# A model's expert stage: the main up projection is ordered behind a rare branch, and the branch hint is issued later

## The chip, the cores and the metric

The kernel runs on one core of one Trainium2 chip. The metric is the device time of one execution, in microseconds (us). PE is TensorE (matmuls; PEld are its weight loads), DVE is VectorE, ACT is ScalarE, POOL is GpSimd, SP is SyncE, whose queue issues the weight transfers here. "PEq" or "SPq" is the instruction queue (the sequencer) of that engine.

## The reference

Two transformer stacks run one after the other on 256 tokens of width 1024. The first has four layers of three kinds of mixers, the second one hybrid mixer and one layer of experts. Only the experts matter here:

```python
def clamped_swiglu(hgu):
    gate, up = jnp.split(hgu, 2, axis=-1)
    gate = jnp.minimum(gate, SWIGLU_LIMIT)
    up = jnp.clip(up, -SWIGLU_LIMIT, SWIGLU_LIMIT)
    return gate * jax.nn.sigmoid(SWIGLU_ALPHA * gate) * (up + 1)

logits = (xt @ w_router + b_router).astype(jnp.float32)
top_v, top_e = lax.top_k(logits, TOP_K)            # 4 of 32 experts for each token
gates = jax.nn.softmax(top_v, axis=-1)
# for each expert e, over the tokens that chose it:
y_e = clamped_swiglu(x @ w1[e] + b1[e]) @ w2[e] + b2[e]     # w1[e]: 1024 x 2048, w2[e]: 1024 x 1024
# the sum over a token's four experts, weighted by its gates, is added to the stream, then a norm
```

With 256 tokens and 4 choices of 32, an expert gets 32 tokens on average; the number depends on the data.

## The kernel before, in words

All of it is one program of straight code. The mixers fill about the first 1300 us; the expert stage (`route`, then `experts`) fills the rest, and the change is there.

**Weights.** An expert's weights are 12 transfers of 1024 KB: eight chunks of `w1` (128 rows each) and four of `w2`. `wload` issues them on SP's queue in a fixed order: the eight of `w1[e+1]`, then the four of `w2[e]`, and so on. They go into a ring of 18 buffers (`SPLIT + sum(RING) + 4`), so each load takes the buffer that was filled 18 loads before, and can start only when the last reader of that buffer is done. Counted through, the loads 3 to 6 of `w1[e+2]` take the buffers of `w2[e-1]`, its loads 7 and 8 those of the first two chunks of `w1[e+1]`, the four of `w2[e+1]` those of chunks 3 to 6 of `w1[e+1]`, and the first two of `w1[e+3]` those of its chunks 7 and 8.

**One expert.** For expert e the code (the loop at L1924) calls `others`, then `up_proj`, the main up projection for the first 64 tokens: 8 chunks x 4 column blocks, 32 matmuls into the sums `hg` (a bias had been written there by `new_hg`). `swiglu` runs on DVE and ACT. Then `down` of the expert before (16 matmuls into `py`), then `between`: the bias of the next expert (4 matmuls on `sel`), `prep` (a gather matmul of the tokens for the next pair of experts, into a tile `g`, whose result DVE and ACT scale into `xq`; at odd experts also slot gates and transposes of `P`), and `act_T`, four transposes of the activation. At even experts a `scatter` of 8 matmuls adds the pair's result to the stream.

**The branch.** Tokens beyond the 64th of an expert are rare. `others(e)` (L1895) is a runtime branch on the number `more`: its body does the down projection of the rest of expert e-2 and the up projection of the rest of expert e, with further conditions inside. The body reads `w1[e]` and `w2[e-2]` once more. Each engine takes the branch for itself: it loads the number into a register and jumps over the body where it is 64 or less. `branch_ahead` (L1705) places the load, and for PE a hint that this jump is coming; it is called in `down_proj`, behind the matmul `kk == hh == 0`, for the expert after the next.

**What sets the order.** A scheduler orders each engine's instructions by their dependences. `up_proj` does not depend on the body (the body writes other sums, the two tiles `hg0` and `hg1`), and so the scheduler may put its matmuls ahead of the branch, and does. A buffer counts as free behind its last reader in the program: for a chunk that is read by `up_proj` ahead of the branch that is the body, and so the branch's end.

Of the kernel before, what the change touches and what calls it, by code (L numbers as in the profile page):

```python
# [51 lines left out]
def tile_model(ctx: ExitStack, tc: tile.TileContext, A, out):  # L52
# [18 lines left out]
    ps = psst.enter_context(tc.tile_pool(name="ps", bufs=2, space=PSUM))  # L71
# [8 lines left out]
    ident = cb[:, 0:128]  # L80
# [54 lines left out]
    def mm(o, l, r, start=True, stop=True):  # L135
        return T.matmul(o, l, r, start=start, stop=stop)  # L136
# [1271 lines left out]
    def w2_tile(e, kk, hh):  # L1408

        if e < 31:  # L1410
            return w2s[e][kk // 2][:, kk % 2, hh * 512:(hh + 1) * 512]
        return w2s[e][2 * hh + kk // 4][:, kk % 4, :]
# [138 lines left out]
    def slices(j):  # L1551
        return slice(64 * j, 64 * j + 64)
# [3 lines left out]
    def block(hg, b):  # L1556
        if len(hg.shape) == 2:
            return hg[32 * b:32 * b + 32, :], 32
        return hg[64 * (b % 2):64 * (b % 2) + 64, b // 2, :], 64
# [10 lines left out]
    def ytile():  # L1570
        return rt["pe"].tile([128, 512], F32, name="py", tag="py", bufs=2)
# [58 lines left out]
    def experts(pos, gate, num, more):  # L1630
        h = xc
        with ExitStack() as st:
# [30 lines left out]
            def onehots(P, e, s0=0):  # L1663

                for t in range(2):
                    at = pos[:, t, e:e + 1]
                    if s0:
                        ats = ep.tile([128, 1], F32, name="ats", tag="ats")
                        V.tensor_scalar(ats, at, -float(s0), None, ALU.add)
                        at = ats  # L1670
                    V.tensor_scalar(P[:, t], slots, at, None, ALU.is_equal)  # L1671

            def gather(P, n, dst, ks, ps=None):

                w = n * 64
                step = min(512 // w, ks[1] - ks[0])
                for k0 in range(ks[0], ks[1], step):
                    p = (gtile() if ps is None else ps).rearrange("p (a b) -> p a b", b=w)
                    for t in range(2):
                        for k in range(k0, k0 + step):  # L1680
                            mm(p[:, k - k0, :], h[:, t, k * 128:(k + 1) * 128], P[:, t, :], t == 0 and k == k0, t == 1 and k == k0 + step - 1)
                    modulate(dst[:, k0:k0 + step, :], p, range(k0, k0 + step))
# [19 lines left out]
            def branch_ahead(after, i):  # L1702

                with tc.issue_after(after.ins):
                    conds[i] = nc.values_load(more[0:1, i - 1:i], min_val=0, max_val=256)  # L1705
                    tc.mark_branch_hint_location(f"more{i}", "LikelyTaken", [mybir.EngineType.PE])

            def up_proj(w1, hg, xs, k0=0, k1=8):
                for k in range(k0, k1):
                    for b in range(4):  # L1710
                        i = mm(block(hg, b)[0], xs[:, k, :], w1[k][:, b * 512:(b + 1) * 512], False, k == 7)
                return i
# [17 lines left out]
            def down_proj(aT, e, gs, take):  # L1730

                p = ytile()
                for kk in range(8):
                    for hh in range(2):
                        i = T.matmul(p[64 * hh:64 * hh + 64, :], aT[:, kk % 4, 64 * (kk // 4):64 * (kk // 4) + 64],  # L1735
                                     w2_tile(e, kk, hh), start=kk == 0, stop=kk == 7)
                        if kk == hh == 0:
                            branch_ahead(i, e + 2)
                for hh in range(2):
                    sl = slice(hh * 512, (hh + 1) * 512)  # L1740
                    rs = slice(64 * hh, 64 * hh + 64)
                    take(sl, p[rs, :], gs[rs], g2[rs])
                return i
# [12 lines left out]
            def new_P1():  # L1756
                return ep.tile([128, 512], F32, name="P1", tag="gm")[:, 0:128].rearrange("p (a b) -> p a b", b=64)
# [8 lines left out]
            def gather_more(e, j, ps):  # L1766
                P1 = new_P1()
                onehots(P1, e, 64 * j)
                gather(P1, 1, xs1, (0, 8), ps)

            def up_more(e, hgs, g, k0=0, k1=8):
                if k0 == 0:
                    bias(e, hgs[g])
                up_proj(w1s[e], hgs[g], xs1[:, :, 32 * g:32 * g + 32], k0, k1)

            def act_more(hgs, g, um):
                swiglu(hgs[g][0:64], hgs[g][64:128], um[half(g)], half(g))
# [46 lines left out]
            def prepare_sum(q):  # L1824
                gs = ep.tile([128, 2], F32, name="gsq", tag="gsq", bufs=2)
                slot_gates(Pq[q], 2 * q, gs)
                gTs[q] = (twice(30, F32R) if q == 15 else new_gT(F32R), gs)
                if q < 15:
                    transposed(Pq[q], gTs[q][0])
# [33 lines left out]
            def count(e):  # L1863
                return nc.values_load(num[0:1, e:e + 1], min_val=0, max_val=256)

            def down_others(e, ps):

                n, ums = count(e), umss[e % 2]
                with tc.If(n > 64):
                    down_more(e, 1, 0, ums[:, 0], ps)  # L1870
                    with tc.If(n > 96):
                        down_more(e, 1, 1, ums[:, 0], ps)
                        with tc.If(n > 128):
                            for j in (2, 3):
                                for g in range(2):
                                    down_more(e, j, g, ums[:, j - 1], ps)

            def up_others(e, ps):

                n, ums = count(e), umss[e % 2]  # L1880
                with tc.If(n > 64):
                    gather_more(e, 1, ps[1])
                    up_more(e, ps, 0)
                    act_more(ps, 0, ums[:, 0])
                    with tc.If(n > 96):
                        up_more(e, ps, 1)
                        act_more(ps, 1, ums[:, 0])
                        with tc.If(n > 128):
                            for j in (2, 3):
                                gather_more(e, j, ps[1])  # L1890
                                for g in range(2):
                                    up_more(e, ps, g)
                                    act_more(ps, g, ums[:, j - 1])

            def others(i, downs, ups):  # L1895

                ps = [pe.tile([128, 512], F32, name=f"hg{g}", tag=f"hg{g}") for g in range(2)]
                m = conds[i] if i else count(0)
                with tc.If(m > 64, label=f"more{i}"):
                    for e in downs:  # L1900
                        down_others(e, ps)
                    for e in ups:
                        up_others(e, ps)

            umss = [ep.tile([128, 3, 512], F32, name=f"ums{i}", tag=f"ums{i}") for i in range(2)]

# [16 lines left out]
            hg = rt["hg"]  # L1923
            for e in range(32):  # L1924
                while len(w1s.get(e, ())) < 8:
                    wload()
                others(e, (e - 2,) if e > 1 else (), (e,))
                i = up_proj(w1s[e], hg, xq[e // 2][:, :, slices(e % 2)])
                if e == 0:
                    prepare_sum(0)  # L1930
                    branch_ahead(i, 1)
                um = ep.tile([128, 512], F32, name="um", tag="um")
                swiglu(hg[:, 0], hg[:, 1], um)
                def between():

                    nxt = new_hg(e + 1) if e < 31 else None
                    if e < 30:
                        prep(e // 2 + 1, e % 2)
                    return nxt, act_T(um)

                if e == 0:
                    hg, aT = between()
                else:
                    last = down(e - 1, aT)
                    with tc.issue_after(last.ins):
                        hg, aT = between()
                    if e % 2 == 0:
                        scatter(gTs.pop(e // 2 - 1)[0], yes.pop(e // 2 - 1))
                    if e == 20:
                        add_b2()  # L1950
                    if e == 30:
                        ends = prepare_end()
# [33 lines left out]
            ps = [ytile() for _ in range(2)]  # L1986
            prod(0, range(8), ps[0])

            hg = rt["pe"].tile([128, 2, 512], F32, name="hg", tag="hg")
# [11 lines left out]
            i = V.scalar_tensor_tensor(yl[:, 1], ps[1], gs[:, 1:2], g2f[:, 512:1024], ALU.mult, ALU.mult)  # L2001
# [21 lines left out]
    r = route()  # L2023
    ph1.close()
    experts(*r)


# [182 lines left out]
```

## Time and profile before

| | us |
|---|---|
| median of 3 runs (lowest, highest) | 2420.92 (2414.31, 2422.75) |
| the profiled execution, device time | 2417.13 |
| its span | 2415.3 |
| PE busy in the span | 2259.0 (94%) |
| DVE, ACT, POOL busy | 1186.6, 725.8, 81.4 |

PE is busy 94% of the span. A matmul's busy time overlaps its neighbours', so that lengths of work are better read from one start to the next. The mean granted TensorE clock over the span is 0.967 of full speed. In all, 576 MB are moved, nearly all of them weights.

### The profile page before, as it was taken

To read this page: it belongs to the slowest core of one execution; us is meant where nothing else is said; L and a number is where in the kernel's file an instruction comes from. 1 tells how busy PE (TensorE), PEld (TensorE's weight loads), DVE (VectorE), ACT (ScalarE), POOL (GpSimd) and SP (SyncE) were. 2 spreads that over 40 slices of the span, in tenths; PEclk is the share of its full clock that TensorE was granted. 3 is DMA by queue.
4 is the path that set the end of the run, shared out by engine and by line. 5 is a ranking of instruction groups with operands and counts; after the bars stand their busy time and mean duration, and the time that the engine had idled before them with its cause. 6 is when DMAs were issued, how large, how long until landed. Compare 5 with 4: busy or idle time off the path is not lost. (4 is left out here: it accounts for less than half of the span.)

```text
span 2415.3 us, 32552 instructions
## 1 busy us (share of the span) xinstructions
PE 2259.0 (94%) x12508; PEld 1360.8 (56%) x12508; DVE 1186.6 (49%) x2549; ACT 725.8 (30%) x1588; POOL 81.4 (3%) x125
## 2 busy tenths in 40 slices
PE   7999999999999999999999999997988988998887
PEld 4767777777788887668865343332433333433332
DVE  4877666656666668867544323232322333432223
ACT  3545454444333455654223101010110101111001
POOL 0000010000000010002200000000000000000000
PEclk9999999999999999999989999898999989999999
DMA  8443432333333245456227978696999868999996
GB/s 304 131 144 131 135 119 74 108 134 110 118 105 112 81 129 187 167 198 244 82 89 285 413 301 348 263 366 241 416 415 415 332 276 326 367 416 416 415 380 247
DMA packets 124792, 576.08 MB, mean 239 GB/s; under 512 B 11953, under 2 KB 12721, under 8 KB 91762
## 3 DMA queue, kind: packets, MB, share of 16 engines
q1 hardware_dynamic: 124530, 572.71, 62.2%
q8 instruction: 149, 2.44, 0.4%
q14 instruction: 113, 0.93, 0.1%
HBM read 571.61 MB, written 1.05 MB: 237 GB/s over the span
## 5 line engine op out<-in xcount | busy, mean ns | idle before, releaser
L136 PE MATMUL hg<-w,xq 128*64 128x512 f32 x2048 | 505.7, 607 | 42.6 <-DMA w<-w 20.1
L136 PE MATMUL mm<-hT,wp 128*128 128x256 f32 (+1 forms) x1776 | 352.9, 342 | 0.5 <-DVE aqk L144 0.5
L136 PEld LDWEIGHTS hg<-w,xq 128*64 128x64 f32 x2048 | 149.4, 138 | 328.7 <-issue 290.9
L136 PEld LDWEIGHTS mm<-hT,wp 128*128 128x128 f32 x1776 | 270.1, 190 | 64.0 <-issue 27.8
L1735 PE MATMUL py<-w,aT 128*64 128x512 f32 x992 | 230.3, 599 | 20.7 <-DMA w<-w 20.7
L111 DVE TENSOR_TENSOR wp<-w,wp 128x1024 fp32r<-128x1024 f32 (+2 forms) x149 | 178.1, 1200 | 67.1 <-ACT wp L110 66.0
L1716 DVE TENSOR_SCALAR gm<-hg 128x512 f32<-128x512 f32 (+1 forms) x37 | 25.5, 690 | 372.0 <-PE hg L136 369.8
L136 PE MATMUL mm<-wp,hT 128*128 128x256 f32 (+1 forms) x1584 | 199.2, 284 | 4.0 <-DVE mixT L406 2.5
L136 PEld LDWEIGHTS mm<-wp,hT 128*128 128x128 f32 x1584 | 192.0, 190 | 11.9 <-DVE mixT L406 2.7
L110 ACT ACTIVATE wp<-w 128x1024 fp32r<-128x1024 f32 (+2 forms) x149 | 153.8, 1035 | 86.2 <-PE mm L136 57.7
L1735 PEld LDWEIGHTS py<-w,aT 128*64 128x64 f32 x992 | 80.1, 138 | 167.7 <-issue 122.5
L1717 ACT ACTIVATE um<-gm 128x512 f32<-128x512 f32 x32 | 20.2, 630 | 441.0 <-DVE gm L1716 441.0
L136 PE MATMUL ada<-w,scT 128*32 128x512 f32 x576 | 117.7, 620 | 8.0 <-DMA w<-l_w_ada 4.5
L110 ACT ACTIVATE yeh<-gm 64x512 fp32r<-64x512 f32 x62 | 39.0, 629 | 259.8 <-DVE gm L1856 259.6
L1856 DVE SCALAR_TENSOR_TENSOR gm<-py,gsq,g 64x512 f32<-64x512 f32 x62 | 46.5, 750 | 130.8 <-PE py L1735 129.7
L136 PEld LDWEIGHTS g<-P,xc 128*128 128x128 f32 x496 | 57.8, 191 | 13.8 <-issue 13.8
L136 PE MATMUL g<-P,xc 128*128 128x128 f32 x496 | 63.8, 281 | 1.7 <-DVE P L1671 1.7
L136 PE MATMUL hg<-w,xs 128*32 128x512 f32 x480 | 62.0, 671 | 3.4 <-DVE xs L144 2.8
L136 PE MATMUL s<-wp,oz 128*128 128x512 f32 x264 | 64.2, 392 | 0.0
L136 PEld LDWEIGHTS s<-wp,oz 128*128 128x128 f32 x264 | 49.1, 188 | 13.4 <-issue 2.5
L574 ACT ACTIVATE e<-e,nm 128x512 f32<-128x512 f32 x64 | 45.7, 716 | 29.9 <-DVE nm L573 29.7
L111 DVE TENSOR_TENSOR yel<-gm,yeh 64x512 fp32r<-64x512 f32 x60 | 41.2, 686 | 24.9 <-ACT yeh L110 23.7
(608 smaller groups left out, 3039.5 us busy)
## 6 DMA issues: line engine op xcount, KB each, us to landing
w<-w SPq DMA_DIRECT2D x383, 1024.0 KB, 18.1
w<-l_w_ada SPq DMA_DIRECT2D x96, 512.0 KB, 4.4
w<-w_ada SPq DMA_DIRECT2D x48, 512.0 KB, 4.1
w<-l_w_z SPq DMA_DIRECT2D x32, 512.0 KB, 4.5
w<-l_w_out SPq DMA_DIRECT2D x32, 512.0 KB, 4.3
w<-l_w_q SPq DMA_DIRECT2D x16, 512.0 KB, 5.2
w<-l_w_v SPq DMA_DIRECT2D x12, 512.0 KB, 5.2
w<-w_dqkv SPq DMA_DIRECT2D x12, 512.0 KB, 4.4
```

The costliest lines, as they stand in the source:

```text
L110: S.activation(hi, src, AF.Copy)
L111: V.tensor_tensor(lo, src, hi, op=ALU.subtract)
L136: return T.matmul(o, l, r, start=start, stop=stop)
L574: S.activation(e, e, AF.Exp, scale=0.125, bias=nm[:, c:c + 1], accum_out=den[:, c:c + 1])
L1716: V.tensor_scalar(gm, gate, 7.0, None, ALU.min)
L1717: S.activation(um, gm, AF.Sigmoid, scale=1.702)
L1735: i = T.matmul(p[64 * hh:64 * hh + 64, :], aT[:, kk % 4, 64 * (kk // 4):64 * (kk // 4) + 64], w2_tile(e, kk, hh), start=kk == 0, stop=kk == 7)
L1856: V.scalar_tensor_tensor(w, p, gs, g2, ALU.mult, ALU.mult)
```

## The change

The main up projection gets a dependence on the branch's body. `up_others` is given the main sums `hg`, and in its body four small matmuls add a product to one column of each of the four blocks of `hg`. The product is of two elements of the identity matrix, `ident[0, 1]` (which is 0) and `ident[0, 0]`, so that it adds zero. Since the body now writes `hg`, the scheduler has to keep all 32 matmuls of `up_proj` behind the branch; `up_proj` is then the last reader of the chunks of `w1[e]`, and the branch's end is so only for `w2[e-2]`. The second edit moves the place at which `branch_ahead` is called in `down_proj` from the first of the 16 matmuls to the seventh (`kk == 3`, `hh == 0`).

```diff
                         i = T.matmul(p[64 * hh:64 * hh + 64, :], aT[:, kk % 4, 64 * (kk // 4):64 * (kk // 4) + 64],
                                      w2_tile(e, kk, hh), start=kk == 0, stop=kk == 7)
-                        if kk == hh == 0:
+                        if kk == 3 and hh == 0:
                             branch_ahead(i, e + 2)
...
-            def up_others(e, ps):
+            def up_others(e, ps, hg):
 
                 n, ums = count(e), umss[e % 2]
                 with tc.If(n > 64):
+                    for b in range(4):
+                        mm(block(hg, b)[0][:, 0:1], ident[0:1, 1:2].to_broadcast([1, 64]), ident[0:1, 0:1], False, False)
                     gather_more(e, 1, ps[1])
...
-            def others(i, downs, ups):
+            def others(i, downs, ups, hg=None):
...
-                        up_others(e, ps)
+                        up_others(e, ps, hg)
...
-                others(e, (e - 2,) if e > 1 else (), (e,))
+                others(e, (e - 2,) if e > 1 else (), (e,), hg)
```

PE's order, at the start of an expert of odd number (expert 11), from the branch's end to the down projection. `hg<-w,xq` is the main up projection, `py<-w,aT` the down projection. Before:

```order
L1899 UNCONDITIONAL_BRANCH x2
L136 MATMUL hg<-w,xq 64x512 x4
L1735 MATMUL py<-w,aT 64x512
L2206 BRANCH_PREFETCH_HINT
L1735 MATMUL py<-w,aT 64x512 x15
```

and now:

```order
L1901 UNCONDITIONAL_BRANCH x2
L136 MATMUL hg<-w,xq 64x512 x32
L1735 MATMUL py<-w,aT 64x512 x7
L2208 BRANCH_PREFETCH_HINT
L1735 MATMUL py<-w,aT 64x512 x9
```

Four matmuls of the up projection were left behind the branch, now all 32 are; the hint stands six down matmuls later.

PE's order at the end of the same expert, from the gather to the next branch. `g<-P,xc` is the gather, `g<-gate,P` the slot gates, `g<-cb,P` the transposes of P, `g<-cb,um` those of `act_T`. Before:

```order
L136 MATMUL g<-P_20765,xc 128x128 x8
L136 MATMUL g<-gate,P_20765 64x1 x8
L136 MATMUL hg<-w,xq 64x512 x3
L1688 MATMUL g<-cb,P_20765 128x128 x2
L136 MATMUL hg<-w,xq 64x512
L1726 MATMUL g<-cb,um 128x128 x4
L136 MATMUL hg<-w,xq 64x512 x24
L1705 TENSOR_LOAD more
L1899 COMPARE_AND_BRANCH
```

and now:

```order
L136 MATMUL g<-P_20809,xc 128x128 x8
L136 MATMUL g<-gate,P_20809 64x1 x8
L1688 MATMUL g<-cb,P_20809 128x128 x2
L1726 MATMUL g<-cb,um 128x128 x4
L1705 TENSOR_LOAD more
L1901 COMPARE_AND_BRANCH
```

The 28 up matmuls of the next expert that stood between these steps and ahead of the branch are gone from here.

## Rows read from the trace of the kernel before

**Rows 1.** The page, the span in 40 slices: DMA busy tenths and GB/s.

```profile
DMA  8443432333333245456227978696999868999996
GB/s 304 131 144 131 135 119 74 108 134 110 118 105 112 81 129 187 167 198 244 82 89 285 413 301 348 263 366 241 416 415 415 332 276 326 367 416 416 415 380 247
```

**Rows 2.** Stretches: length, busy time of each engine, PE clock, DMA share, GB/s.

```profile
1625.00:1645.00 20.00, 14.91 (x97) 4.92 (x98) 7.23 (x18) 0.77 (x2) 0.00 (x0) 0.91 0.18 76
...
2100.00:2300.00 200.00, 183.00 (x882) 71.28 (x880) 60.55 (x106) 21.62 (x40) 0.00 (x0) 0.98 1.02 416
```

**Rows 3.** PE's waits, 1300 to 2416 us: waited for, us in total, times, longest.

```profile
PE py L1735 <- DMA w<-w: 20.7, 37, 0.7
PE hg L136 <- DMA w<-w: 20.1, 15, 10.1
PE hg L136 <- DVE ats L1669: 11.8, 3, 5.8
PE hg L136 <- PEq L1899: 10.6, 17, 4.9
```

**Rows 4.** SP queue's waits, 1180 to 2416 us, same columns.

```profile
SPq L1392 <- PEq L1899: 210.2, 22, 21.3
```

**Rows 5.** PE in time, experts 10 and 11: start, us, operation, count, [idle before].

```profile
1685.02 1.94 PE L136 MATMUL hg<-w,xq 128*64 128x512 f32 x8 [0.45 <-PEq L1899]
...
1712.89 1.94 PE L136 MATMUL hg<-w,xq 128*64 128x512 f32 x8 [0.30 <-PEq L1899]
1714.63 7.07 PE L1735 MATMUL py<-w,aT 128*64 128x512 f32 x32
1721.50 0.63 PE L136 MATMUL hg<-b1p,sel 96*64 96x512 bf16 x4
...
1724.05 0.63 PE L136 MATMUL g<-gate,P 128*64 128x1 f32 x16
1724.53 1.91 PE L136 MATMUL hg<-w,xq 128*64 128x512 f32 x6
...
1728.33 10.52 PE L136 MATMUL hg<-w,xq 128*64 128x512 f32 x48
1739.31 1.94 PE L136 MATMUL hg<-w,xq 128*64 128x512 f32 x8 [0.46 <-PEq L1899]
```

**Rows 6.** PE in time, two down chunks of expert 15.

```profile
1831.69 2.04 PE L1735 MATMUL py<-w,aT 128*64 128x512 f32 x8 [0.59 <-DMA w<-w]
1834.13 1.94 PE L1735 MATMUL py<-w,aT 128*64 128x512 f32 x8 [0.39 <-DMA w<-w]
```

**Rows 7.** PE in time, behind the taken branch of expert 9.

```profile
1656.47 3.68 PE L136 MATMUL hg<-w,xq 128*64 128x512 f32 x8 [10.07 <-DMA w<-w]
```

**Rows 8.** DVE in time, expert 11, behind its gather.

```profile
1725.08 0.15 DVE L1698 COPY gsq<-g 128x2 f32<-128x2 f32 x1
...
1726.02 0.40 DVE L1496 TENSOR_SCALAR xq<-g,modA,modB 128x128 f32<-128x128 f32 x1
```

**Rows 9.** PE in time, experts 0 and 1.

```profile
1309.82 8.80 PE L136 MATMUL hg<-w,xq 128*64 128x512 f32 x38
...
1327.58 2.02 PE L136 MATMUL g<-P,xc 128*128 128x128 f32 x16 [1.69 <-DVE P L1671]
...
1332.60 0.63 PE L1726 MATMUL g<-cb,um 128*128 128x128 f32 x4 [0.45 <-PEq L1899]
```

**Rows 10.** PE in time, the first and the third taken up branch.

```profile
1428.43 0.38 PE L136 MATMUL hg<-b1p,sel 96*32 96x512 bf16 x1 [3.35 <-DVE ats L1669]
...
1865.41 0.59 PE L136 MATMUL hg<-b1p,sel 96*32 96x512 bf16 x1 [5.85 <-DVE ats L1669]
```

**Rows 11.** PE in time, behind the skipped branch of expert 25.

```profile
2188.98 3.68 PE L136 MATMUL hg<-w,xq 128*64 128x512 f32 x8 [4.92 <-PEq L1899]
2192.42 7.50 PE L1735 MATMUL py<-w,aT 128*64 128x512 f32 x32
```

## The prediction

> **What bounds the kernel now.** The row of GB/s in the page's 40 slices comes first [rows 1]: the expert stage begins in slice 22, and in seven of its slices the transfers run at 413 to 416 GB/s and no higher. The busy shares by stretch give the same ceiling and beside it an exception: from 1625 to 1645 the transfers moved 76 GB/s, a share of 0.18 [rows 2]. An expert is 12 transfers of 1024 KB, 12.58 MB, so at 416 GB/s it takes 30.2 us. The PE timeline gives the other side: from the first up matmul of expert 10 to that of expert 12 it is 1739.31 - 1685.02 = 54.3 us, 27.1 an expert, with no transfer waited for [rows 5]. So an expert whose rare branch is skipped is 3.1 us longer for the transfers than for PE. In the PE timeline seven of the 33 branches are taken, the last at expert 20; there PE is the longer, and the ring fills up. Behind it twelve experts live on what the ring holds. PE's waits say what that costs: 20.7 us in 37 waits of the down projection and 20.1 in 15 of the up projection [rows 3]. Of the second sum 10.07 is one wait behind a taken branch [rows 7], in the stretch where the transfers stood at 0.18. I read it as the jump out of the body and not as a transfer, which leaves 30.7. SP's queue, last, waits 210.2 us in 22 waits for the branch [rows 4]: the loads stand behind it while they have room to run.
>
> **The change part by part.**
>
> *Loads earlier.* 28 of the 32 up matmuls leave the place ahead of the branch. 48 records, 24 matmuls, last 10.52 us with the end of the last [rows 5], from start to start some 0.43 each, so the branch's end comes 28 x 0.43 = 12.0 us sooner against PE's need. The chunks of `w1[e]` then come free one by one. What can be won is the 30.7 us, and what pacing costs beyond the waits: two down chunks of expert 15 start 1834.13 - 1831.69 = 2.44 us apart, of which 0.39 is the wait [rows 6]. Of 32 records that take 7.07 us [rows 5], eight take 1.77, so 0.28 is lost beyond the wait. At 0.2 in each of 52 waits that is 10 us: 41 at most. What stays: the twelve last experts lack 12 x 3.1 = 37 us, less 9 by which PE grows longer (next term), 28. Six buffers beyond one expert's twelve are 6 x 2.5 = 15 us of loads when the ring is full; with the 12.0 that is 27. Bounds for the rest are 0 and 28 - 12 = 16; I take 3, near the lower, since the ring is full behind a taken branch. Term: **-38** (-41 to -25).
>
> *Cover lost.* These 28 matmuls also filled PE while DVE and ACT worked. At expert 11 the down projection's issue ends at 1721.50, four bias matmuls, gather and slot gates follow, and the gates go from 1724.05 for about 0.5 us [rows 5]. Now the transposes of `P` come at once and wait for the copy `gsq`, at 1725.08 + 0.15 [rows 8]; `act_T` needs a buffer of `g` that `xq` reads, 1726.02 + 0.40 on DVE and its other half on ACT some 0.4 behind. So `act_T` starts near 1726.9, with 0.6 for it; the branch is over and the up projection starts at about 1728.1, 6.6 us behind the down's issue. Before, the same stretch without the up matmuls was 1739.31 - 1721.50 = 17.8, less 28 x 0.43 = 12.0, 5.8. That is +0.8 at an odd expert; at an even one the scatter waits similarly, +0.6. Over 30 experts: **+21**. Below, the mixing of up matmuls and steps costs something that goes away: six records took 1.91 there and would take 6 x 0.215 = 1.29 [rows 5], -0.6 an expert, -18; above, if DVE and ACT begin later than drawn, 2 us each, +60. I stay with the drawn chain, which rests on DVE's own rows.
>
> *Start.* Experts 0 and 1 have the longest cover, 38 records in 8.80 us at 1309.82, and behind it a wait of 1.69 for `P` [rows 9]; now both the wait and branch 0, which has no hint, are open, and the first `act_T` is 0.63 at 1332.60 as before. **+4** (2 to 7).
>
> *Taken branches.* Into a branch that does only the up part PE jumps over the down part. Three such rows are put down to DVE's `ats`, 11.8 us in all [rows 3], among them 3.35 and 5.85 [rows 10]. Where up matmuls were still queued they hid a piece of it; now none are. Three at 5.85 are 17.6, +5.8; four down branches at about +1 each: **+10** (0 to 18).
>
> *Zeros.* Four matmuls of one column in each of four taken up branches; no row shows one. The nearest is the gates' matmul, 16 records in 0.63 [rows 5], 0.04 each: 32 records, **+1** (0 to 3).
>
> *Hint later.* It stands seven matmuls into the down projection instead of one, and the branch 28 matmuls nearer. Before, it led by 1739.31 - 1714.63 = 24.7 us less a first matmul. Now nine down matmuls, 9/16 x 7.07 = 4.0, and the 6.1 that the chain above takes to the end of `act_T` (1727.6 - 1721.5): some 10 us. With 24.7 us of lead 16 of the 17 stops at the branch are short, 10.6 - 4.92 = 5.7 in all, such as 0.30 and 0.45; one, at expert 25, was 4.92, and behind it the clock was at its lower level: 3.68 for eight records against 1.94, and 7.50 for the down against 7.07 [rows 3, 5, 11]. So a late jump is 4.92 + 1.74 + 0.4, about 7 us. Nothing shows how often 10 us is too short. The bounds are -7 (the one late jump goes) and +170 (25 more); I take one more, as the only late one in the trace lasted 4.92 us, less than the 10 there are: **+7**.
>
> [...]
>
> Sum: -38 + 21 + 4 + 10 + 1 + 7 = **+5** against the profiled execution's 2417.1, that is 2422. The median of the runs is 3.8 above that execution, so 2426 as a median.
>
> **The rivals.**
>
> *Cover not missed (faster).* The steps run as fast without the up matmuls between them, since what the mixing itself cost comes back; the 21 falls to about -5. For it: the 1.91 for six records. Against it: DVE's rows, by which `xq` is done 1.9 us behind the last gate. 2426 - 26 = 2400; to 2392 if the taken branches cost nothing too.
>
> *Hints too late (slower).* PE reaches the branch before the jump's target is there, the stop is 4.92 and the clock falls with it. Its place is the stop at the branch, its price 7 us, and it decides from two late jumps more than counted (2426 + 14 = 2440); five more give 2461, eight 2482, all 25 nearly 2600. For it: one was late at 24.7 us of lead, so lead alone isn't safety. Against it: sixteen were in time, with a lead that is now a third.
>
> *The waits stay (slower).* Four loads of `w1[e+2]` still wait for `w2[e-1]`, which is free at a branch's end only, before and after; they stand in the one queue ahead of the others. If they hold the queue, the 12 us buy little, and three quarters of the 38 stay as waits: 2426 + 28 = 2454. Against it: that branch's end itself comes 12 us earlier.
>
> **How the numbers follow.** A measurement of this kernel tells about 0.3% from no change, 7 us: 2413.7 to 2428.2. The forecast, a sum near zero of a gain and several losses of like size, has a chance of 0.45, in its own range of 2406 to 2442: 0.13 faster, 0.20 the same, 0.12 slower. Cover not missed 0.20, all faster. Hints too late 0.23 and waits that stay 0.12: slower but for 0.04 that end within the bound, when gains elsewhere are larger. That makes 0.33 faster, 0.24 the same, 0.43 slower. The range, 2394 to 2474, leaves out the lowest edge of the fast case and more than seven late jumps.
>
> **What would show it.** In the profile after, PE's waits for `w` should be under 8 us but for one jump out of a body, and SP's queue should wait less for the branch. The pair of experts 10 and 11 should take about 55.7 us, with waits for DVE's copies ahead of the transposes, the scatter and `act_T`; at 53 the cover wasn't needed. The stops at the branch, their number over 3 us and rows of 3.68 behind them settle the hints. The first up row should come near 1310 as now and expert 2's 4 us later. The forecast is wrong if the waits for `w` stay above 20 us, or if more than three jumps are late.

## The result, and the profile after

The changed kernel takes 2448.36 us (median; 2445.79 to 2458.03), the kernel before on the same chip 2417.61. The ratio is 1.0124, 95% interval 1.0096 to 1.0151: slower, by some 31 us. The forecast was 2426, about no change, with a range of 2394 to 2474.

PE's waits of the changed kernel, 1300 us to the end (waited for, us in total, times, longest):

```profile
PE hg L136 <- PEq L1881: 22.5, 3, 10.6
PE hg L136 <- PEq L1869: 18.9, 3, 7.2
PE hg L136 <- PEq L1901: 12.3, 24, 2.9
PE py L136 <- ACT yeh L110: 8.7, 14, 1.0
PE g L1688 <- DVE gsq L1698: 8.5, 14, 0.6
PE py L136 <- DVE xl L1753: 7.5, 14, 0.5
PE g L1726 <- DVE gTq L144: 6.5, 6, 1.1
PE g L1726 <- PEq L1901: 6.3, 1, 6.3
PE py L1735 <- DMA w<-w: 5.1, 9, 0.7
...
PE hg L136 <- DMA w<-w: 1.3, 2, 0.7
```

Against [rows 3], the waits put down to weights went from 40.8 us, of which 10.07 are a jump (shown below), to 6.4: the change does what it says. Three groups came in their place: jumps of the taken branches (L1881, out of a body, and L1869, over the down part), small waits for DVE and ACT between the down projection and the branch (`yeh`, `gsq`, `xl`, `gTq`), and one stop of 6.3 at a branch.

SP's queue, from 1180 us, same columns; against [rows 4] it waits less for the branch (210.2 before), and now in many pieces for the up projection's matmuls, which free the chunks one by one (18.6 us in 12 waits before):

```profile
SPq L1392 <- PE hg L136: 197.0, 84, 25.6
SPq L1392 <- PEq L1901: 172.1, 19, 23.6
```

PE in time, experts 10 and 11 (start, us, operation, count, [idle before]), which answer to [rows 5]:

```profile
1696.63 0.60 PE L136 MATMUL hg<-b1p,sel 96*64 96x512 bf16 x4
...
1700.39 0.44 PE L1688 MATMUL g<-cb,P 128*128 128x128 f32 x2 [0.62 <-DVE gsq L1698]
1701.91 0.66 PE L1726 MATMUL g<-cb,um 128*128 128x128 f32 x4 [1.08 <-DVE gTq L144]
1703.01 15.58 PE L136 MATMUL hg<-w,xq 128*64 128x512 f32 x64 [0.44 <-PEq L1901]
...
1733.02 13.95 PE L136 MATMUL hg<-w,xq 128*64 128x512 f32 x64 [0.42 <-PEq L1901]
...
1753.64 0.63 PE L136 MATMUL hg<-b1p,sel 96*64 96x512 bf16 x4
...
1758.33 0.66 PE L1726 MATMUL g<-cb,um 128*128 128x128 f32 x4 [0.47 <-ACT gTq L142]
1759.51 1.08 PE L136 MATMUL hg<-w,xq 128*64 128x512 f32 x4 [0.52 <-PEq L1901]
```

From the end of a down projection (1696.63) to the next up projection (1703.01) it is 6.4 us, and one pair later (1753.64 to 1759.51) 5.9, where 6.6 had been drawn. From the up projection of expert 10 to that of expert 12 it is 56.5 us, foreseen as 55.7. But the up projection of expert 10 takes 15.58 us, and the next one 13.95. The stretches show why (length, busy time of PE, PEld, DVE, ACT and POOL with the number of records in brackets, PE clock, DMA share, GB/s):

```profile
1700.00:1703.00 3.00, 1.09 (x6) 0.64 (x7) 2.32 (x9) 1.68 (x4) 0.00 (x0) 0.99 1.00 415
1703.00:1706.00 3.00, 2.99 (x8) 1.10 (x10) 0.00 (x0) 0.20 (x1) 0.00 (x0) 0.50 0.86 276
1706.00:1709.00 3.00, 3.00 (x16) 0.96 (x14) 0.00 (x0) 0.00 (x0) 0.00 (x0) 0.95 1.02 423
```

PE was busy 1.09 of 3 us, and in the next three its clock is granted at 0.50, the lower level: 8 matmul records instead of 16. No single gap there is over 1.08 us. Behind expert 11's between, where the copy `gTq` is made by ACT and the wait is 0.47 instead of 1.08, the clock stays at 1.00. That is no rule: ahead of expert 22's up projection, which starts at 2128.43, the waits are 0.60, 1.08 and 0.42, nearly those of expert 10, and the clock is granted in full, 1.00:

```profile
2125.40:2128.40 3.00, 1.09 (x6) 0.62 (x7) 2.36 (x9) 1.68 (x4) 0.00 (x0) 1.00 1.05 419
2128.40:2131.40 3.00, 2.97 (x14) 1.26 (x16) 0.00 (x0) 0.24 (x1) 0.00 (x0) 1.00 1.05 423
```

Behind scatters, waits of about 0.35, 0.60 and 0.54 are followed by 0.51 at experts 19 and 23, and by 1.00 at expert 11. So the lower clock followed such gaps at some experts and not at others; what decides it stays open. Seven up projections behind skipped branches (experts 3, 10, 14, 19, 23, 26 and 30) start at the lower clock (0.50 or 0.51 in the first 3 us) and run 15.58 to 16.46 us for 64 records, against 13.95 at 1.00; those of experts 2 and 31 start at 0.54 and 0.60.

The start, which answers to [rows 9]:

```profile
1314.54 15.26 PE L136 MATMUL hg<-w,xq 128*64 128x512 f32 x64 [2.85 <-PEq L1901]
1332.70 0.62 PE L136 MATMUL hg<-b1p,sel 96*64 96x512 bf16 x4 [2.90 <-DVE um L1719]
1339.67 1.09 PE L1726 MATMUL g<-cb,um 128*128 128x128 f32 x4 [6.35 <-PEq L1901]
```

Branch 0 stops PE for 2.85 us and branch 1 for 6.35. The hint for branch 1 stands behind expert 0's up projection. By the rows that projection now ends 3.5 us ahead of the branch (1329.80 to 1333.32) and ended 7.0 ahead of it before (1325.10 to 1332.15). That the stop is long for this reason is a reading: no run moved this hint alone.

One taken branch into the up part and one out of the down part; rows of before are [rows 10]:

```profile
1436.62 0.58 PE L136 MATMUL hg<-cb 1*64 1x1 f32 x8 [6.84 <-PEq L1869]
...
1532.57 15.47 PE L136 MATMUL hg<-w,xq 128*64 128x512 f32 x64 [10.63 <-PEq L1881]
```

### The profile page after: what moved, and what is told of

It is laid out like the page before. It is cut to its first block, busy times and chain, and to the rows that moved or that the text cites. A ratio compares the mean times of both kernels' runs of the same rounds, so it can differ in the third digit from the quotient of the medians.

```text
span 2443.9 us, 32737 instructions
## 1 busy us (share of the span) xinstructions
PE 2242.4 (92%) x12540; PEld 1383.1 (57%) x12540; DVE 1184.9 (48%) x2549; ACT 726.4 (30%) x1588; POOL 80.9 (3%) x125
## 5 line engine op out<-in xcount | busy, mean ns | idle before, releaser
L136 PE MATMUL hg<-w,xq 128*64 128x512 f32 x2048 | 473.3, 620 | 39.3 <-PEq L1881 22.5
L136 PEld LDWEIGHTS hg<-w,xq 128*64 128x64 f32 x2048 | 168.0, 143 | 331.4 <-issue 321.0
L1716 DVE TENSOR_SCALAR gm<-hg 128x512 f32<-128x512 f32 (+1 forms) x37 | 25.5, 690 | 521.9 <-PE hg L136 521.9
L1735 PE MATMUL py<-w,aT 128*64 128x512 f32 x992 | 223.6, 594 | 5.4 <-DMA w<-w 5.1
L136 PEld LDWEIGHTS mm<-wp,hT 128*128 128x128 f32 x1584 | 191.9, 190 | 11.8 <-DVE mixT L406 2.7
L136 PE MATMUL hg<-w,xs 128*32 128x512 f32 x480 | 68.0, 726 | 4.6 <-DVE xs L144 4.0
L136 PEld LDWEIGHTS s<-wp,oz 128*128 128x128 f32 x264 | 49.1, 188 | 13.4 <-issue 2.5
```

Source lines behind the costliest of these rows:

```text
L1716: V.tensor_scalar(gm, gate, 7.0, None, ALU.min)
```

## The experiments

The part of the program ahead of the experts ends up to 14 us apart from one profiled execution to another. So stage lengths, each from the one profiled execution of a kernel, are compared beside the medians: from the row `hg<-modg,cb`, shortly ahead of the first expert, to the span's end, and inside it to the first row of the down projections of experts 0 and 19 (all seven taken branches lie between these two), all from PE's timeline. The labels in the table are explained behind it.

| kernel | median, us | ratio to before on its chip | stage | to down 0 | down 0 to 19 | down 19 to end |
|---|---|---|---|---|---|---|
| before | 2417.61 | | 1110.1 | 40.9 | 693.7 | 375.5 |
| changed | 2448.36 | 1.0124 (1.0096 to 1.0151) | 1140.9 | 53.4 | 720.7 | 366.8 |
| hint_only | 2420.10 | 1.0013 (0.9993 to 1.0033) | 1110.4 | 40.9 | 693.2 | 376.3 |
| zero_only | 2446.07 | 1.0126 (1.0098 to 1.0154) | 1138.7 | 52.0 | 717.3 | 369.3 |
| no_zero_01 | 2425.04 | 1.0022 (0.9998 to 1.0046) | 1115.6 | 40.9 | 705.1 | 369.6 |
| split4 | 2408.48 | 0.9972 (0.9949 to 0.9996) | 1099.5 | 45.5 | 684.9 | 369.1 |
| split2 | 2410.12 | 0.9959 (0.9938 to 0.9980) | 1102.4 | 49.5 | 687.8 | 365.1 |
| split2_01 | 2404.34 | 0.9938 (0.9920 to 0.9955) | 1089.3 | 40.9 | 681.5 | 366.9 |
| split4_01 | 2396.46 | 0.9911 (0.9887 to 0.9935) | 1087.3 | 40.9 | 677.6 | 368.8 |
| before_light | 2361.06 | 0.9742 (0.9716 to 0.9767) | 1052.9 | 43.2 | 669.6 | 340.0 |
| after_light | 2439.57 | 1.0072 (1.0046 to 1.0098) | 1132.1 | 56.6 | 710.8 | 364.7 |
| split4_01_light | 2356.83 | 0.9720 (0.9682 to 0.9757) | 1047.0 | 41.9 | 664.9 | 340.2 |
| shift | 2458.31 | 1.0142 (1.0105 to 1.0179) | 1151.0 | 66.7 | 714.4 | 369.9 |
| shift_half | 2463.95 | 1.0170 (1.0146 to 1.0195) | 1153.0 | 59.0 | 719.1 | 374.9 |

**The two edits apart.** First the hint alone, in the kernel before:

```diff
-                        if kk == hh == 0:
+                        if kk == 3 and hh == 0:
                             branch_ahead(i, e + 2)
```

> The kernel before with only the hint moved to the seventh down matmul, the up projection where it was. Theory (the loss comes from the up projection's order): 2418, within 5 us of before, no more than one skipped branch with a stop over 3 us. Rival (the later hint costs): at least half of the 31 us, 2435 or more, with more stops over 3 us at L1899 or at the jumps inside the body.

Then the zeros alone, with the hint where it was:

```diff
-                        if kk == 3 and hh == 0:
+                        if kk == hh == 0:
                             branch_ahead(i, e + 2)
```

> The changed kernel with the hint back at the first down matmul. Theory: as the changed kernel, 2448 +- 5. Rival (the later hint costs): 2433 or less. A third view, that the hint has to move with the branch and its new place saves time: 2455 or more, with several stops over 3 us at skipped branches.

With the hint alone the time is that of before, with the zeros alone that of the change, both times by interval. The hint's place costs nothing that can be measured and gives nothing; behind expert 1 no skipped branch of the changed kernel stops PE for over 1 us. For the skipped branches the rival "hints too late" falls.

hint_only also settles a reading. In it the first row behind the taken branch of expert 9, which in [rows 7] has 10.07 us put down to a transfer, reads:

```profile
1660.79 3.68 PE L136 MATMUL hg<-w,xq 128*64 128x512 f32 x8 [4.44 <-PEq L1881]
```

It is a jump, as the DMA share of 0.18 had suggested, and its length isn't fixed.

**The start.** The zeros are left out for experts 0 and 1:

```diff
-                others(e, (e - 2,) if e > 1 else (), (e,), hg)
+                others(e, (e - 2,) if e > 1 else (), (e,), hg if e > 1 else None)
```

> The changed kernel without the zero matmuls for experts 0 and 1, so that their up projections may stand ahead of branches 0 and 1 again. Theory (the start's 10.3 us come from these two experts): 2438 to 2441, first down matmul near 1346 instead of 1356. Rival (these stops only move to the next expert): 2446 or more.

The way to the first down projection is 40.9 us again, 12.5 less, as before to 0.1. The total fell by more than expected, 23 us, since another 15.6 went between down 0 and 19. There the code behind expert 1 is unchanged, but the three jumps out of a body take 12.4 us instead of 22.5:

```profile
PE hg L136 <- PEq L1881: 12.4, 3, 4.4
```

With that the kernel takes as long as before, by interval, though from expert 2 on all 32 matmuls stand behind the branch.

**Do jumps hang on their place in the program?** Small matmuls are put ahead of the first expert, 64 and then 32:

```diff
+            p = gtile()
+            for _ in range(64):
+                mm(p[0:64, 0:1], ident[0:1, 1:2].to_broadcast([1, 64]), ident[0:1, 0:1])
             hg = rt["hg"]
```

> The changed kernel with 64 more small matmuls (0.04 us each, 2.7 in all) ahead of the first expert, so that all that follows stands 128 instructions later in PE's program; nothing else moves. Theory (how long PE stops at a jump inside or out of a taken body hangs on where the jump stands in the program): the three stops at L1881, 22.5 us in the changed kernel and 12.4 in the one without zeros for experts 0 and 1, change by 5 us or more in sum, and the time with them, 2436 to 2448. Rival (these stops are long because the cover is gone): each within 1 us of the changed kernel's, 2451.

> The changed kernel with 32 more small matmuls ahead of the first expert instead of 64, half the shift. With 64 the three stops at L1881 came out as in the changed kernel (9.88, 1.72, 10.24), so either the place in the program doesn't matter or the shift of 64 gave each jump the same place in a pattern that repeats. Theory (a repeating pattern): two of the three stops differ from 10.6, 1.7, 10.2 by 3 us or more, 2440 to 2452. Rival (place doesn't matter): all within 1 us of these, 2452 +- 5.

With 64 the stops are the changed kernel's 10.63, 1.72 and 10.21 again to within 0.8, and the first expectation, that they change, failed. With 32 they are others, as the second expectation had it. Both times came out above what either view expected. The same rows behind the taken branches of experts 6, 9 and 20, of shift, its 64 matmuls first:

```profile
1308.55 11.34 PE L136 MATMUL g<-cb 1*64 1x1 f32 x128
...
1543.17 7.29 PE L136 MATMUL hg<-w,xq 128*64 128x512 f32 x24 [9.88 <-PEq L1881]
...
1682.48 15.72 PE L136 MATMUL hg<-w,xq 128*64 128x512 f32 x63 [1.72 <-PEq L1881]
...
2069.74 15.41 PE L136 MATMUL hg<-w,xq 128*64 128x512 f32 x64 [10.24 <-PEq L1881]
```

and of shift_half, its 32 matmuls first:

```profile
1315.35 3.89 PE L136 MATMUL g<-cb 1*64 1x1 f32 x64
1315.35 3.80 PEld L136 LDWEIGHTS g<-cb 1*64 1x64 f32 x64
...
1536.34 13.90 PE L136 MATMUL hg<-w,xq 128*64 128x512 f32 x50 [4.06 <-PEq L1881]
...
1685.47 14.87 PE L136 MATMUL hg<-w,xq 128*64 128x512 f32 x60 [4.36 <-PEq L1881]
...
2072.16 16.94 PE L136 MATMUL hg<-w,xq 128*64 128x512 f32 x64 [4.03 <-PEq L1881]
```

The first two rows of shift_half correct the expectations: a small matmul is two records, each with a weight load, so 32 of them are 128 instructions and 64 are 256; with the 32737 that the changed kernel's page counts, that makes 32865 in shift_half and 32993 in shift. Nor are they cheap: 64 take 11.34 us instead of 2.7, with a granted clock of 0.66 from 1310 to 1315 and 0.50 from 1315 to 1320, and the way to the first down projection is 13.3 us longer than in the changed kernel, with 32 it is 5.6. A shift by 256 gave each of the three jumps out of a body its old length to within 0.8 us, one by 128 did not. That the lengths are no chance of one execution shows in zero_only and after_light, whose PE programs differ from the changed kernel's in the hint's place and in which half of `w2` is read: the three stops are 21.8 and 22.1 there, against 22.5. Two runs are too few to show that the lengths repeat with the place. Nothing was won by the shift of 128: the three stops lost 9.4 us, but others came, such as 5.1 at a skipped branch near the end, and the time was no better than with 64. So some 10 us of such stops sit in one build and not in another, and single stops of one kernel are no measure of a change.

**How much the transfers give and the order costs.** In both kernels half of each `w2` load is left out from expert 2 to 30; the down projection reads the loaded half twice. An expert then loads 10.5 MB, and no longer waits for it:

```diff
+                n = 2 if e < 2 else 1
+                nc.sync.dma_start(t[:, 0:n], A["w2_2"][e, c * 256:c * 256 + 128 * n, :].rearrange("(a p) d -> p a d", p=128))
...
-        return w2s[e][kk // 2][:, kk % 2, hh * 512:(hh + 1) * 512]
+        return w2s[e][kk // 2][:, kk % 2 if e < 2 else 0, hh * 512:(hh + 1) * 512]
```

> The kernel before with half of each w2 load left out from expert 2 to 30 (the down projection reads the loaded half twice), so that an expert's transfers are 10.5 MB, 25.2 us. It says what the waits for weights cost there. Theory: waits for w all but vanish, 30.7 us and the pacing of some 10: 2375 to 2387. Rival (they hide waits of other kinds that then show): 2400 or more.

> The changed kernel with the same half loads left out. Theory (its waits for w are already gone): 2436 to 2446, within 12 us of the changed kernel, so that without the transfers' bound the change costs some 60 us. Rival (the transfers still bound its end): 2425 or less.

PE's waits of before_light:

```profile
PE hg L136 <- DMA w<-w: 9.9, 1, 9.9
PE hg L136 <- PEq L1900: 8.5, 24, 0.5
PE hg L136 <- PEq L1882: 8.0, 2, 4.6
PE hg L136 <- DVE ats L1670: 7.8, 4, 2.3
```

and of after_light:

```profile
PE hg L136 <- PEq L1882: 22.1, 3, 10.2
PE hg L136 <- PEq L1870: 13.8, 3, 5.0
PE hg L136 <- PEq L1902: 12.7, 24, 3.6
PE py L136 <- ACT yeh L110: 8.7, 14, 1.0
PE g L1689 <- DVE gsq L1699: 8.5, 14, 0.6
PE py L136 <- DVE xl L1754: 7.5, 14, 0.5
PE g L1727 <- PEq L1902: 6.4, 1, 6.4
PE g L1727 <- DVE gTq L144: 5.4, 5, 1.1
...
PE py L136 <- DVE yel L111: 4.6, 8, 0.6
...
PE g L1727 <- ACT gTq L142: 3.3, 7, 0.5
```

The 9.9 put down to a transfer is again the jump out of expert 9's body. By stage, the bytes left out cost the kernel before 1110.1 - 1052.9 = 57.2 us and the changed one 8.8: the earlier release is worth 48.4. Where transfers no longer bound the kernel, the change costs 1132.1 - 1052.9 = 79.2. The difference is the 30.8 between the two stages. The medians say much the same: before_light is 60.7 us below before, after_light 78.5 above before_light. Both numbers are larger than the prediction's, and before_light is faster than expected (2361 against 2375 at the least). Why the transfers cost before more than the waits for weights show is seen in the jumps: the late one of [rows 11] isn't there in before_light (no stop over 0.5 at L1900), and the jumps into the up part take 7.8 us in four (`ats`) instead of 14.6 in four, 11.8 in three put down to `ats` and 2.8 in one put down to `P`.

**A part of the cover given back.** The first four (or two) of the eight chunks are written ahead of the branch:

```diff
-                i = up_proj(w1s[e], hg, xq[e // 2][:, :, slices(e % 2)])
+                ahead = 4
+                up_proj(w1s[e], hg, xq[e // 2][:, :, slices(e % 2)], 0, ahead)
+                others(e, (e - 2,) if e > 1 else (), (e,), hg)
+                i = up_proj(w1s[e], hg, xq[e // 2][:, :, slices(e % 2)], ahead)
```

> The changed kernel with the first four chunks of each main up projection (16 matmuls) written ahead of the branch and the last four behind it. Theory (the loss is lost cover and the gain is an earlier release): most of the cover and some 60% of the release come back, 2405 to 2420, PE's waits for w under 15 us, few stretches at the lower clock between skipped experts. Rival (any up matmul ahead of the branch gives the waits back in proportion): waits for w near 20 us and about 2430, half way between the two kernels.

> Two chunks (8 matmuls) of each main up projection ahead of the branch, six behind it. Theory (8 matmuls, 3.4 us, cover most of the small waits in the between, and the release comes earlier than with four chunks): waits for w under 15 us, at most 3 experts at the lower clock behind a skipped branch, 2400 to 2410. Rival (what decides behind the last taken branch is the transfers, whatever the order): same as four chunks, 2408 +- 5, with the length from the end of the last taken branch to the end again 379 to 386 us.

Both are faster than before by interval, by 0.3% and 0.4%. The waits for weights are 25.5 and 18.2 us, more than expected (under 15), and still the times came, split2's 0.1 us above its range: 8 or 16 matmuls are enough for the between. But split2's rival, the same time as split4's, came as well. With split4 the pair of skipped experts from down 9 to down 11 takes 54.2 us, with split2 54.1, where before took 54.3 and the changed kernel 56.0.

Experts 0 and 1 as in no_zero_01, and `ahead` 2 or 4 from expert 2 on:

> Two chunks of each main up projection ahead of the branch, and experts 0 and 1 as in the kernel before (all ahead, no zeros). Theory (start and cover add up): first down matmul 41 us behind the stage's start instead of 49.5, 2400 to 2405 in the median, the best so far. Rival (the transfers set the end, so that the 8.6 us are waited away behind the last taken branch): 2408 to 2412, with a length behind that branch above 385.

> The same with four chunks ahead of the branch. Theory: 4.6 us less at the start than with zeros for all experts, 2402 to 2406. Rival (given back behind the last taken branch): 2407 to 2411.

These are the fastest, 0.6% and 0.9% below before; both reach the first down projection 40.9 us behind the stage's start, as expected, and split4_01 gained more than expected in all. Against each other they can't be told apart: the intervals overlap, and of the profiled executions split2_01's is the shorter. How much of the gain is the order's isn't shown. Of the 22.8 us by which split4_01's stage is shorter, 7.1 lie in the interval of expert 9, where the jump out of the body takes 1.73 us instead of 10.07, and such lengths move with the build (4.44 in hint_only, 4.39 in split2_01). From the up projection of expert 20 to the end both take about as long, 378.2 and 378.8 us. What is shown is that the cover is kept: at all 24 stops at a skipped branch the three us behind it are at the full clock, 1.00, though two of these stops last 1.55 and 1.61. The between of split4_01 at expert 10, with the up matmuls as filler and no wait for DVE or ACT:

```profile
1690.92 0.40 PE L136 MATMUL py<-yel,gTq 128*128 128x512 f32 x1
1691.25 1.07 PE L136 MATMUL hg<-w,xq 128*64 128x512 f32 x2
1692.26 0.49 PE L136 MATMUL py<-yeh,gTq 128*128 128x512 f32 x1
1692.68 1.08 PE L136 MATMUL hg<-w,xq 128*64 128x512 f32 x4
1693.69 0.49 PE L136 MATMUL py<-yel,gTq 128*128 128x512 f32 x1
```

Last, split4_01 with the same half loads left out as above:

> Four chunks ahead of the branch, experts 0 and 1 as before, and half of each w2 load left out from expert 2 to 30. Theory (16 matmuls cover the between as well as 28, and only what is left of the waits for weights separates this kernel from one without them): 2350 to 2366, as the light kernel before (2361), no up projection between skipped experts at the lower clock. Rival (half the cover is lost with half the matmuls): 2385 or more, a half of the 79 us between the two light kernels.

It is as fast as before_light: where transfers don't bound it, the order with 16 matmuls ahead costs nothing (the start kept as before). Of the three light kernels only the one with all 32 behind the branch, from expert 0 on, shows the 79 us.

## Why the prediction was right, and where not

The range held, and the direction with the largest chance came (slower, 0.43); the forecast itself, a sum near zero, was 22 us too low, and 2448 lies outside the 2406 to 2442 that it was given for its own. Of the 0.43 for slower, 0.31 came from two rivals that the runs refute, so that the direction came right is in part luck. Step by step:

- *Loads earlier, -38:* right in kind, measured -48. The waits went to 6.4 us, as foreseen (under 8). What was missed is that with the transfers' bound jumps go too or get shorter, as before_light shows (into the up part 7.8 us instead of 14.6, and the late one of 4.92 gone); but the late one is gone in hint_only too, with all loads (no stop over 1.9 at L1899), so it needn't have gone for that reason.
- *Cover lost, +21:* mis-sized, and the largest miss in us. The drawn chain held, 6.4 us against 6.6, and DVE's and ACT's copies are what PE waits for, 38 us in the rows of after_light shown. Of that, a part is given back by what mixing had cost, so that the gaps alone come near the 0.6 that was taken for an even expert: from down 9 to down 10, behind an up projection at the full clock, it is 28.36 us against 27.87 before. Not foreseen was the clock. The gaps were priced by their length; but some are followed by the lower clock, 0.50, for some 3 us of the next up projection, 1.6 to 2.5 us more for seven of them. In the light pair the 23 intervals without a taken branch, with the end of the kernel, cost 42.4 us (the 79.2 less the next two points), 8.5 of them in the interval that ends at expert 30's down projection. Read from the timeline of after_light, nine of its up projections (experts 3, 10, 11, 14, 15, 19, 23, 26 and 30) start below the full clock and take 0.8 to 2.5 us longer than the 13.75 at the full clock, 14.0 in all, a third of the 42.4; how the rest splits wasn't tried apart.
- *Start, +4:* mis-sized, 12.5 (13.4 light). The step that failed is that branch 1 was counted as hinted, as before, though its hint's matmul now ends 3.5 us ahead of it: a stop of 6.35 us instead of 0.45, though no run shows that the short lead makes it. Behind it expert 1's up projection starts at a clock of 0.50 and takes 15.84 us. Nor could the first up row come near 1310 "as now": it stands behind branch 0, 11.6 us behind the stage's start instead of 4.6.
- *Taken branches, +10:* mis-sized. Into the up part, L1869 and L1871 take 22.7 us in four (18.9 in three, and one of 3.8) against 14.6 in four before, 8.1 more where 5.8 was worked out. With 8 matmuls ahead (split2) the three at L1869 take 13.7 and with 16 (split4) 8.9, as the working has it, by which queued matmuls hide a piece of them. Out of the down part, which had been counted at +1 each, two stops are 10.6 and 10.2, where before has 3.3 and 4.4 and, the other way, 10.07 against 1.72 at expert 9. Over the seven intervals with a taken branch the light pair differs by 23.4 us. The three stops out of a body make 4.2 of that, 22.1 against 17.9. Their lengths hang on the build in both kernels: they are 12.4 in no_zero_01 and 12.3 in hint_only, so some 10 us of the changed kernel's, and 5 of those before, are no effect of the order.
- *Zeros, +1:* 0.58 us in the row shown, and much the same in the other three, 2.3.
- *Hint later, +7:* nothing either way.

So the sum of the costs was 43 and measured 79, the gain 38 and measured 48. Among the rivals, "cover not missed" and "the waits stay" are refuted, and so is "hints too late" for the skipped branches; stops of the kind that it described stand at the two branches of the start and inside the taken ones, though no run shows that the target was late there.

## What to carry to other kernels

Work that is moved behind a rare branch to free its buffers was also filler for what stands ahead of the branch; keep as much of it ahead as the waits there are long (here 8 to 16 matmuls of 32) and move the rest. Price a row of short gaps on TensorE by the clock that may follow it (here 0.50 for some 3 us behind some such rows, 1.00 behind others) as well as by its length. Before single stops at jumps are put down to a change, build the kernel again with its code shifted: they move with the build (here the same jump took 10.07 us in one and 4.44 in another).

## What the runs showed of the hardware

- A stretch in which PE was busy 1.09 of 3 us, with no gap over 1.08, was followed by about 3 us at the lower clock, 0.50, at expert 10; one with nearly the same gaps, at expert 22, by the full clock, 1.00. In split4_01 single stops of 1.55 and 1.61 were followed by 1.00 as well.
- Jumps over the down part of a taken body took longer with the full loads than with half of `w2` left out, in all three pairs: 14.6 us in four against 7.8 before, 18.9 in three against 13.8 for the change, 8.8 in three against 5.9 for split4_01.
- The same jump at the same place in the program took 10.07 us in one build and 4.44 in another that differed in the hint alone.
- 64 matmuls of one column, 256 instructions, put ahead of the experts left all three jumps out of a body as long as they were, to within 0.8 us; 32 of them, 128 instructions, changed all three by 2.6 us or more.
